# Moving the start addresses of weight and token tiles in a split-precision encoder layer on one Trainium2 core

## The chip, the core and the metric

The kernel runs on one core of one Trainium2 chip. TensorE (PE in the profile) multiplies matrices, and each of its matmuls has a weight load (PEld) ahead of it. VectorE (DVE), ScalarE (ACT) and GpSimd (POOL) work on elements, SyncE (SP) issues most of the DMAs. The operands of all of them lie in SBUF, a memory of 128 partitions; a tile has the same byte address in each partition. Sums of matmuls are collected in PSUM.

The metric is the device time of one execution in microseconds, as the median of some runs.

## The reference: what is computed

One encoder layer (D_MODEL 2048) for two groups of tokens that share all weights: a prompt of 256 and a sample of 32, 288 together.

```python
xn = rmsnorm(x, norm_mix_pre)
u, z, xbc, dt = split(xn @ w_in)              # 1024 | 2048 | 2560 | 32 columns
y_pool = pool_mixer(u)                        # trailing means, w_pool, pool_scale
y_ssd = ssd_mixer(z, xbc, dt)                 # convolution, chunked scan, gate, norm
x = x + rmsnorm(concat[y_pool, y_ssd] @ w_out, norm_mix_post)
up = causal_dwconv(rmsnorm(x, norm_ffn_pre) @ w_up)      # 2 * 5632 columns
x = x + rmsnorm((silu(gate) * value) @ w_down, norm_ffn_post)
```

Outputs are the two new `x` and the new states of pooling, convolutions and scan. All data is float32.

## The kernel before

**Layout.** Features lie on the partitions, the 288 tokens along the free axis. A projection is a sum over blocks of 128 features: the stationary operand is a 128x128 piece of a weight tile, the moving operand a token tile of 128x288.

**Split precision.** TensorE gets rounded operands (`float32r`), so each operand is split into a rounded high part and the rest. A token tile `a` has shape [128, 2, 288]: half 0 is the high part, half 1, which starts 1152 bytes later, the rest. `split_w` (L134) splits a weight tile of 1024 columns: ACT writes `whi` (L146), DVE subtracts and writes `wlo` (L147). `mm3` (L162) then issues three matmuls for each 128x128 piece and 288 tokens:

```python
pe.matmul(out, wh, a[:, 0, :], start=start, stop=False)   # L163
pe.matmul(out, wh, a[:, 1, :], start=False, stop=False)   # L164
pe.matmul(out, wl, a[:, 0, :], start=False, stop=stop)    # L165
```

**Order of the work.** `project` (L167) runs a projection: it fetches raw weights by SP (L131), splits them, and issues the matmuls. The stages follow each other: w_in (token tiles `xn`, about 7 to 337 us of the span), w_pool and w_out (`du`, `mixp`, `mixs`, to 506 us), a normalisation of the whole token axis (about 506 to 550 us), w_up (`hn`) and the two halves of w_down (`fa`), to 1360 us, and the output. Inside w_in and w_out lies the work of the mixers. The narrow 32 columns of `dt` go through `split_narrow` (L151), where high part and rest stand side by side in one 64-column weight piece (L187, L188). A scheduler orders the instructions of each engine when the program is built, from its own model of time.

**Where tiles lie.** The pools are laid out one after the other: `const` (small constants, among them `scan_one` 1152 bytes, `sel`, `pick` and `sel64`, L229 to L239), `wpool` (4 buffers each of `raw`, `whi`, `wlo`), `shift` (one tile of 128 bytes that nothing uses), `apool` (16 token tiles of 2304 bytes), `bpool` (20 tiles of 1152 bytes), and then the pool of a stage (`xin`, `mixer`, `outp` or `ffn`). In the built program every `whi` and `wlo` buffer starts at 224 modulo 256. Buffers are 4096 bytes apart and pieces 512 bytes, so every 128x128 weight piece starts there too. Half 0 of every token tile of the projections (`xn`, `mixs`, `mixp`, `du`, `hn`, `fa`) starts at 96, and half 1 at 224 modulo 256. SBUF is full to 32 bytes in the largest stage.

**Two smaller places.** `state_out` (L684) writes the mixer's states through a tile `so` of its own (L689). The FFN's new state leaves through a tile `fso` (L969).

Of the kernel before, what the change touches and what calls it, by code (L numbers as in the profile page):

```python
# [8 lines left out]
F32 = mybir.dt.float32  # L9
F32R = mybir.dt.float32r  # L10
AF = mybir.ActivationFunctionType
ALU = mybir.AluOpType
AX = mybir.AxisListType
# [3 lines left out]
P = 128  # L17
# [4 lines left out]
NT = NP_ + NS  # L22
# [3 lines left out]
HEADS = 32  # L26
# [3 lines left out]
NX = D_SSD // P  # L30
NF = D_FF // P
# [12 lines left out]
def body(  # L44
# [38 lines left out]
    act, dve, pool, pe, sp = nc.scalar, nc.vector, nc.gpsimd, nc.tensor, nc.sync  # L83
# [10 lines left out]
    const = ctx.enter_context(tc.tile_pool(name="const", bufs=1))  # L94
    wpool = ctx.enter_context(tc.tile_pool(name="wpool", bufs=4))
# [8 lines left out]
    def aux(shape, name):  # L104
        return aux_ps.tile(shape, F32, tag="aux", name=name)
# [4 lines left out]
    def btile(name):  # L110
        return bpool.tile([P, NT], F32, tag="b", name=name)

    def split_from(a, src, scale=None):
# [4 lines left out]
        else:  # L118
# [4 lines left out]
                ),  # L123
            )

    ahead = [0]

    def fetch_w(view, kb, nk, c0, nc_):
# [5 lines left out]
    def split_w(raw, kb, nk, nc_, after=()):  # L134

        out = []
        step = min(nk, 1024 // nc_)
        for k in range(0, nk, step):
            n = min(step, nk - k)
            hi = wpool.tile([P, n, nc_], F32R, tag="hi", name="whi")  # L140
            lo = wpool.tile([P, n, nc_], F32R, tag="lo", name="wlo")
            with ExitStack() as order:
                order.enter_context(tc.high_priority(offset=ahead[0]))
                for ins in after:
                    order.enter_context(tc.issue_after(ins.ins))
                act.activation(hi, raw[:, k : k + n, :], AF.Copy)  # L146
                dve.tensor_tensor(lo, raw[:, k : k + n, :], hi.bitcast(F32), op=ALU.subtract)  # L147
            out.append([(kb + k + i, hi[:, i, :], lo[:, i, :]) for i in range(n)])
        return out
# [17 lines left out]
    def project(view, groups, acts, ksplit, before=None, done=None, spare=0, hold=()):  # L167
# [9 lines left out]
        for i, (kb, n) in enumerate(ksplit):  # L177
            raws = [fetch_w(view, kb, n, c0, w) for c0, w in groups]
            nxt = None
            if before and i + 1 < len(ksplit):  # L180
                nxt = before(*ksplit[i + 1])
            m0 = 0
            for raw, (c0, w) in zip(raws, groups):
                if w < P:
                    for k, both in split_narrow(raw, kb, n, w, after or ()):
                        o = accs[m0][: 2 * w, :]
                        pe.matmul(o, both, acts[k][:, 0, :], start=k == k_first, stop=False)  # L187
                        pe.matmul(o, both, acts[k][:, 1, :], start=False, stop=k == k_last)  # L188
                    continue
                parts = split_w(raw, kb, n, w, ((after or ()) if m0 else ()) + (hold if i else ()))  # L190
                for q, part in enumerate(parts):
                    for m in range(w // P):
                        c = slice(m * P, (m + 1) * P)
                        for k, hi, lo in part:
                            mm3(accs[m0 + m], hi[:, c], lo[:, c], acts[k], k == k_first, k == k_last)
                        if done and i + 1 == len(ksplit) and q + 1 == len(parts):
                            done(m0 + m, accs[m0 + m])
                m0 += w // P
            after = nxt
# [13 lines left out]
    ident = const.tile([P, P], F32, name="ident")  # L213
# [12 lines left out]
    rec = const.tile([P, 16], F32, name="rec")  # L226
    for t in range(16):
        pool.memset(rec[:, t : t + 1], 1.0 / (t + 1))
    scan_one = const.tile([HEADS, NT], F32, name="scan_one")  # L229
    pool.memset(scan_one, 1.0)  # L230
    for c in range(0, NT, 64):
        pool.memset(scan_one[:, c : c + 1], 0.0)
    sel = const.tile([HEADS, 2], F32, name="sel")
    pick = const.tile([HEADS, NX], F32, name="pick")
    id32 = ident[:HEADS, :HEADS]
    dve.tensor_reduce(sel, id32.rearrange("h (t r) -> h r t", r=2), axis=AX.X, op=ALU.add)
    dve.tensor_reduce(pick, id32.rearrange("h (t r) -> h t r", r=2), axis=AX.X, op=ALU.add)
    sel64 = const.tile([HEADS, 2, 64], F32, name="sel64")
    dve.tensor_copy(sel64, sel.unsqueeze(2).broadcast_to([HEADS, 2, 64]))  # L239

    NE = 4
    ebuf = []
    for i in range(NE):
# [120 lines left out]

    mixer = ExitStack()
    mp = mixer.enter_context(tc.tile_pool(name="mixer", bufs=1))
    sc_stage = const.tile([P, 2, 3, NXC], F32, name="sc_stage")
    np_stage = const.tile([P, 2, 15, NU], F32, name="np_stage")
    hist_c = pb[:, 0:60].rearrange("p (r t) -> p r t", t=NXC)
# [43 lines left out]
    def htile(name, n=NT, tag=None):  # L413
        return mp.tile([HEADS, n], F32, tag=tag or name, name=name, bufs={"z": 4}.get(tag, 2) if tag else 1)
# [23 lines left out]
    r = htile("r", tag="z")  # L438
# [42 lines left out]
    for i in range(4):  # L481
        o = btile("bc")
# [201 lines left out]
    def state_out(stage, n, outs, pool_):  # L684

        for s in range(2):
            p_ = aux([n, P], "pso")
            pe.transpose(p_, stage[:, s, :], ident)
            o = pool_.tile([P, P], F32, tag="so", bufs=2, name="so")  # L689
            act.activation(o[:n, :], p_, AF.Copy)  # L690
            sp.dma_start(out=outs[s], in_=o[:n, :])

# [46 lines left out]
    def pool_group(i):  # L739
        raw = fetch_w(wpv, 2 * i, 2, 0, 256)  # L740
        wq = split_w(raw, 0, 2, 256)[0]
        for j in range(2):
            o = acc_ps.tile([P, NT], F32, tag="acc", name="acc")
            c = slice(j * P, (j + 1) * P)
            for k, hi, lo in wq:
                mm3(o, hi[:, c], lo[:, c], uin[2 * i + k], k == 0, k == 1)
            a = op_.tile([P, 2, NT], F32R, name=f"mixp{2 * i + j}")
            split_from(a, o, p_scale[:, 2 * i + j : 2 * i + j + 1])
            mix[2 * i + j] = a
# [46 lines left out]
    for gi in range(2):  # L796
        c = slice(gi * P, (gi + 1) * P)
# [46 lines left out]
    for grp in ((0, 1), (2,), (3,), (4,), (5,), (6,), (7,)):  # L844
        project(
            wov, [(256 * c, 256) for c in grp], mix, [(8, 8), (16, 8), (0, 8)],
            mix_before(grp[0]), lambda m, p_: mix_out(p_),
        )
        if grp[0] < 6:
            for t in range(LATE * (grp[0] - 2) // 4, LATE * (grp[0] - 1) // 4) if grp[0] else ():  # L850
                state_mm(t, *state_in(t))
        elif grp[0] == 6:
            late_in = [state_in(t) for t in range(LATE, NX)]
        if grp[0] == 0:
            sp.dma_start(out=xT, in_=xT_d)
            state_out(sc_stage.rearrange("p s r t -> p s (r t)"), 60, (rows4(new_sconv_p), rows4(new_sconv_s)), op_)
            state_out(np_stage.rearrange("p s r t -> p s (r t)"), 120, (rows4(new_pool_p), rows4(new_pool_s)), op_)
# [10 lines left out]
    for s in range(KD + 1):  # L868
# [3 lines left out]
        if s:  # L872
            t = s - 1
            a = atile("hn")
            hi = act.activation(a[:, 0, :], x1[t], AF.Copy, scale=g_ffn_pre[:, t : t + 1])
            lo = dve.scalar_tensor_tensor(  # L876
                a[:, 1, :], x1[t], g_ffn_pre[:, t : t + 1], a[:, 0, :].bitcast(F32),
                op0=ALU.mult, op1=ALU.subtract,
            )
# [16 lines left out]
    fp = ffn.enter_context(tc.tile_pool(name="ffn", bufs=1))  # L896
# [60 lines left out]
    part = []  # L957
    up_half(0, HALF)
    for m in range(0, KD, 2):
        for p_ in project(wdv[:, 0:HALF, :], [(m * P, 256)], f[:HALF], [(0, 8), (8, 8), (16, 6)]):  # L960
            o = btile("part")
# [3 lines left out]
    for s, o_ in enumerate((new_fconv_p, new_fconv_s)):  # L965
        p_ = aux([2 * NF, 2, P], "pfo")
        for r_ in range(2):
            pe.transpose(p_[:, r_, :], fc_stage[:, s, r_, :], ident)
        so = fp.tile([2 * NF, 2, P], F32, tag="fso", bufs=1, name="fso")  # L969
        act.activation(so, p_, AF.Copy)  # L970
        sp.dma_start(out=o_.rearrange("o b r (t p) -> t (o b r) p", p=P), in_=so)

# [6 lines left out]
    for q in range(4):  # L979
        for b in range(2):  # L980
            t = apool.tile([P, 512], F32, tag="a", name="xr")
# [126 lines left out]
```

## Time and profile before

| what | value |
|---|---|
| median of three runs | 1377.21 us (1376.95 to 1377.78) |
| the profiled execution: its own time | 1377.7 us |
| the profiled execution: span from first to last instruction | 1376.0 us |
| granted TensorE clock, mean | 0.994 |
| PE busy | 1355.0 us (98%) |
| DVE busy | 879.3 us (64%) |
| ACT busy | 670.8 us (49%) |
| POOL busy | 240.8 us (18%) |
| HBM read and written | 234.55 MB and 14.31 MB |

A group of the profile reads: line of the kernel, engine, operation, output<-inputs, shapes, count; then busy time in us and mean ns of one; then the idle time just ahead of them and what ended it. Matmuls overlap each other, so the mean duration of one is more than the time from the start of one to the start of the next, which is called the pitch below. A window row gives for a stretch of the span the busy time of each engine with the number of its instructions in brackets, then the granted clock, the DMA share and GB/s.

### The profile page before, as it was taken

Reading aid. Unit: us, or ns where it says so; the run is one execution under the profiler, and the core shown is the slowest. Engines: PE = TensorE matmul, PEld = TensorE weight load, DVE = VectorE, ACT = ScalarE, POOL = GpSimd, SP = SyncE. Lnnn points to the kernel's source line nnn. Section 1 sums busy time; section 2 is a strip of 40 time slices with the busy share of each in tenths; the row PEclk is TensorE's granted clock in tenths of the full one; section 3 lists DMA queues with packets and bytes.
Section 4 is the critical chain, followed back from the end, with each engine's and each line's share of the span. In section 5 each row is a group of like instructions: output and inputs, shape, how many; then the busy total and the mean of one; then the engine's idle time right before and its main releaser. Section 6 shows DMA issues by size and latency. Waiting matters only on the chain.

```text
span 1376.0 us, 25874 instructions
## 1 busy us (share of the span) xinstructions
PE 1355.0 (98%) x10247; PEld 1333.0 (97%) x10247; DVE 879.3 (64%) x1551; ACT 670.8 (49%) x1013; POOL 240.8 (18%) x394
## 2 busy tenths in 40 slices
PE   8999999999999999999999999999999999999996
PEld 7999999999999998999999999999999999999995
DVE  6898887669544448877667653334766766654443
ACT  6547767546444345644444443334444444454441
POOL 3122211122123310212112100000211211201110
PEclk9999999999999999999999999999999999999998
DMA  8878875455755634766555455555555545476662
GB/s 270 258 194 262 250 207 171 152 187 176 228 179 175 191 106 146 223 176 194 175 157 178 149 169 169 169 170 161 176 161 171 167 156 181 155 230 184 191 186 86
DMA packets 293287, 250.55 MB, mean 182 GB/s; under 512 B 67344, under 2 KB 286458, under 8 KB 293038
## 3 DMA queue, kind: packets, MB, share of 16 engines
q1 hardware_dynamic: 289962, 242.41, 57.8%
q0 software_dynamic: 2320, 3.86, 0.9%
q10 hardware_dynamic: 884, 2.63, 0.5%
q8 instruction: 80, 1.31, 0.4%
q14 instruction: 41, 0.34, 0.1%
HBM read 234.55 MB, written 14.31 MB: 181 GB/s over the span
## 4 chain that ended last, share of the span: by engine, by line
PE 97%; DVE 2%; issue 0%; DMA 0%; ACT 0%; DVEq 0%
PE acc L163 31%; PE acc L165 31%; PE acc L164 30%; PE pst L824 1%; PE py L555 1%; DVE wlo L147 0%; DVE xr L1066 0%; DVE hn L876 0%; PE py L559 0%; PE py L561 0%; PE py L557 0%; DVE xsum L888 0%; DMA xt<-in_x_prompt 0%; PE pt L299 0%; PE pt L301 0%
## 5 line engine op out<-in xcount | busy, mean ns | idle before, releaser
L147 DVE TENSOR_TENSOR wlo<-raw,whi 128x1024 fp32r<-128x1024 f32 (+1 forms) x414 | 493.9, 1194 | 351.2 <-ACT whi L146 349.8
L146 ACT ACTIVATE whi<-raw 128x1024 fp32r<-128x1024 f32 (+1 forms) x414 | 427.1, 1033 | 518.6 <-PE acc L164 424.8
L163 PE MATMUL acc<-hn,whi 128*128 128x288 f32 x1392 | 409.0, 297 | 2.3 <-ACT whi L146 2.3
L165 PE MATMUL acc<-hn,wlo 128*128 128x288 f32 x1392 | 410.0, 296 | 0.9 <-DVE wlo L147 0.9
L164 PE MATMUL acc<-hn,whi 128*128 128x288 f32 x1392 | 405.4, 292 | 0.0
L163 PEld LDWEIGHTS acc<-hn,whi 128*128 128x128 f32 x1392 | 260.9, 188 | 3.5 <-ACT whi L146 3.4
L165 PEld LDWEIGHTS acc<-hn,wlo 128*128 128x128 f32 x1392 | 260.9, 188 | 1.9 <-DVE wlo L147 1.8
L164 PEld LDWEIGHTS acc<-hn,whi 128*128 128x128 f32 x1392 | 262.2, 188 | 0.2 <-DVE hn L876 0.2
L163 PE MATMUL acc<-xn,whi 128*128 128x288 f32 x704 | 210.1, 300 | 0.0
L163 PE MATMUL acc<-fa,whi 128*128 128x288 f32 x704 | 208.5, 296 | 0.0
L165 PE MATMUL acc<-fa,wlo 128*128 128x288 f32 x704 | 207.4, 295 | 0.0
L165 PE MATMUL acc<-xn,wlo 128*128 128x288 f32 x704 | 207.0, 296 | 0.0
L164 PE MATMUL acc<-xn,whi 128*128 128x288 f32 x704 | 206.8, 295 | 0.0
L164 PE MATMUL acc<-fa,whi 128*128 128x288 f32 x704 | 205.3, 292 | 0.0
L163 PEld LDWEIGHTS acc<-xn,whi 128*128 128x128 f32 x704 | 132.6, 189 | 0.7
L164 PEld LDWEIGHTS acc<-xn,whi 128*128 128x128 f32 x704 | 132.8, 189 | 0.3
L164 PEld LDWEIGHTS acc<-fa,whi 128*128 128x128 f32 x704 | 132.3, 188 | 0.0
L163 PEld LDWEIGHTS acc<-fa,whi 128*128 128x128 f32 x704 | 132.3, 188 | 0.0
L165 PEld LDWEIGHTS acc<-xn,wlo 128*128 128x128 f32 x704 | 131.9, 188 | 0.3
L165 PEld LDWEIGHTS acc<-fa,wlo 128*128 128x128 f32 x704 | 131.7, 187 | 0.0
L909 POOL COPY fc_stage<-ebuf 128x4 f32<-128x4 f32 x88 | 27.5, 312 | 506.0 <-DVE ebuf L908 506.0
L905 POOL COPY ebuf<-pf 128x2 f32<-128x2 f32 x88 | 74.5, 847 | 117.9 <-DVE fc L915 54.0
(308 smaller groups left out, 1635.0 us busy)
## 6 DMA issues: line engine op xcount, KB each, us to landing
raw<-in_w_up SPq DMA_DIRECT2D x82, 1024.0 KB, 5.1
raw<-in_w_in SPq DMA_DIRECT2D x40, 1024.0 KB, 5.6
raw<-in_w_down SPq DMA_DIRECT2D x32, 1024.0 KB, 5.4
raw<-in_w_out SPq DMA_DIRECT2D x24, 1024.0 KB, 5.4
raw<-in_w_down SPq DMA_DIRECT2D x16, 768.0 KB, 4.6
gb<-g_d SPq DMA_DIRECT2D x8, 832.0 KB, 4.9
raw<-in_w_up SPq DMA_DIRECT2D x12, 512.0 KB, 3.6
raw<-in_w_in SPq DMA_DIRECT2D x6, 512.0 KB, 6.4
```

The lines of the kernel that those rows point to most:

```text
L146: act.activation(hi, raw[:, k : k + n, :], AF.Copy)
L147: dve.tensor_tensor(lo, raw[:, k : k + n, :], hi.bitcast(F32), op=ALU.subtract)
L163: pe.matmul(out, wh, a[:, 0, :], start=start, stop=False)
L164: pe.matmul(out, wh, a[:, 1, :], start=False, stop=False)
L165: pe.matmul(out, wl, a[:, 0, :], start=False, stop=stop)
L555: pe.matmul(y[c, 0:256], xw[:, 0, c], m[:, j, 0:256], start=True, stop=False)
L824: ins = pe.matmul(st[:, o, :], x_, w, start=i != 1, stop=i != 0)
L905: pool.tensor_copy(e[:, 258:260], pf[:, 4:6, i])
L909: pool.tensor_copy(fc_stage[:, :, :, i], e[:, 256:324].rearrange("p (s c) -> p s c", c=34)[:, :, 0:2])
```

## The change

`split_w` takes its tiles from a new helper, which allocates 1088 columns and uses 1024 of them from the 58th on. The buffers are 4352 bytes, 17 times 256, and the used part begins 58 * 4 = 232 bytes into each:

```diff
+    def wtile(part, n, nc_):
+        t = wpool.tile([P, 1024 + 64], F32R, tag=part, name="w" + part)
+        return t[:, 58 : 58 + n * nc_].rearrange("p (k c) -> p k c", k=n)
...
-            hi = wpool.tile([P, n, nc_], F32R, tag="hi", name="whi")
-            lo = wpool.tile([P, n, nc_], F32R, tag="lo", name="wlo")
+            hi = wtile("hi", n, nc_)
+            lo = wtile("lo", n, nc_)
```

Four constants go from `const` to the mixer's pool, and their nine set-up instructions with them, from the program's start to behind the first projection:

```diff
-    scan_one = const.tile([HEADS, NT], F32, name="scan_one")
+    scan_one = mp.tile([HEADS, NT], F32, name="scan_one")
...
-    sel64 = const.tile([HEADS, 2, 64], F32, name="sel64")
+    sel64 = mp.tile([HEADS, 2, 64], F32, name="sel64")
```

Two tiles of their own become uses of buffers that are there for other things:

```diff
-            o = pool_.tile([P, P], F32, tag="so", bufs=2, name="so")
+            o = pool_.tile([P, NT], F32, tag="sq", bufs=2, name="so")[:, :P]
...
-        so = fp.tile([2 * NF, 2, P], F32, tag="fso", bufs=1, name="fso")
+        so = fp.tile([P, NT], F32, tag="fr", bufs=2, name="fso")[: 2 * NF, : 2 * P].rearrange("p (r c) -> p r c", r=2)
```

In the built program `const` is 1760 bytes shorter, and the buffers of `wpool` start at 0 modulo 256. Every 128x128 weight piece of the projections then starts at 232 modulo 256 (before: 224), half 0 of a token tile at 128 (before: 96) and half 1 at 0 (before: 224). The distance from the start of the weight piece to the start of the token half goes, modulo 256, from 128 to 152 for half 0 and from 0 to 24 for half 1. All matmuls, their shapes and their number stay as they are. The order of PE's instructions is the same but for stretches among its instructions 154 to 1367 (the first projection and the mixer) and 2717 to 2752 (four transposes of `state_out` move behind 34 matmuls).

More of the change, by code (lines that the diff above doesn't have):

```diff
@@ L228, in body @@
         pool.memset(rec[:, t : t + 1], 1.0 / (t + 1))
-    scan_one = const.tile([HEADS, NT], F32, name="scan_one")
[L230 to L237, printed above, removed]
-    sel64 = const.tile([HEADS, 2, 64], F32, name="sel64")
-    dve.tensor_copy(sel64, sel.unsqueeze(2).broadcast_to([HEADS, 2, 64]))
     NE = 4
@@ L366, in body @@
     mp = mixer.enter_context(tc.tile_pool(name="mixer", bufs=1))
+    scan_one = mp.tile([HEADS, NT], F32, name="scan_one")
+    pool.memset(scan_one, 1.0)
+    for c in range(0, NT, 64):
+        pool.memset(scan_one[:, c : c + 1], 0.0)
+    sel = mp.tile([HEADS, 2], F32, name="sel")
+    pick = mp.tile([HEADS, NX], F32, name="pick")
+    id32 = ident[:HEADS, :HEADS]
+    dve.tensor_reduce(sel, id32.rearrange("h (t r) -> h r t", r=2), axis=AX.X, op=ALU.add)
+    dve.tensor_reduce(pick, id32.rearrange("h (t r) -> h t r", r=2), axis=AX.X, op=ALU.add)
+    sel64 = mp.tile([HEADS, 2, 64], F32, name="sel64")
+    dve.tensor_copy(sel64, sel.unsqueeze(2).broadcast_to([HEADS, 2, 64]))
     sc_stage = const.tile([P, 2, 3, NXC], F32, name="sc_stage")
```

## The prediction

> **What bounds the kernel now.** I read the chain of work that ended last first, then windows, then the groups by line with shapes kept apart, and at last the timeline of PE.
>
> ```profile
> ## 4 chain that ended last, share of the span: by engine, by line
> PE 97%; DVE 2%; issue 0%; DMA 0%; ACT 0%; DVEq 0%
> ```
>
> PE carries 97% of the chain. The windows say how it is filled:
>
> ```profile
> 50.00:500.00 450.00, 450.00 (x3462) 436.22 (x3461) 315.52 (x604) 246.36 (x422) 107.75 (x146) 1.00 0.65 195
> 500.00:550.00 50.00, 46.71 (x319) 43.46 (x318) 37.45 (x76) 26.09 (x52) 2.51 (x4) 0.97 0.46 141
> 550.00:1360.00 810.00, 810.00 (x6138) 809.96 (x6136) 485.15 (x789) 366.52 (x488) 114.72 (x185) 1.00 0.57 173
> 600.00:700.00 100.00, 100.00 (x758) 100.00 (x758) 69.21 (x126) 46.85 (x63) 16.75 (x31) 1.00 0.60 179
> ```
>
> The first column after the length is PE. From 50 to 500 us and from 550 to 1360 us it is busy without a gap, at a granted clock of 1.00. Only the start, the normalisation at 500 to 550 us and the last 16 us hold anything else. So the time is a number of matmuls times their pitch. The window from 600 to 700 us has nothing on PE but projections: 100 us / 758 = 131.9 ns from one start to the next. The change alters no count, so it moves the time by what the addresses do to 131.9 ns, and by little else.
>
> How many matmuls that is, and what one costs by line:
>
> ```profile
> L165 PE MATMUL acc<-hn,wlo 128*128 128x288 f32 x1392 | 410.0, 296 | 0.9 <-DVE wlo L147 0.9
> L163 PE MATMUL acc<-hn,whi 128*128 128x288 f32 x1392 | 409.0, 297 | 2.3 <-ACT whi L146 2.3
> L164 PE MATMUL acc<-hn,whi 128*128 128x288 f32 x1392 | 405.4, 292 | 0.0
> L163 PE MATMUL acc<-xn,whi 128*128 128x288 f32 x704 | 210.1, 300 | 0.0
> L163 PE MATMUL acc<-fa,whi 128*128 128x288 f32 x704 | 208.5, 296 | 0.0
> L165 PE MATMUL acc<-fa,wlo 128*128 128x288 f32 x704 | 207.4, 295 | 0.0
> L165 PE MATMUL acc<-xn,wlo 128*128 128x288 f32 x704 | 207.0, 296 | 0.0
> L164 PE MATMUL acc<-xn,whi 128*128 128x288 f32 x704 | 206.8, 295 | 0.0
> L164 PE MATMUL acc<-fa,whi 128*128 128x288 f32 x704 | 205.3, 292 | 0.0
> L163 PE MATMUL acc<-mixs,whi 128*128 128x288 f32 x256 | 76.1, 298 | 0.0
> L165 PE MATMUL acc<-mixs,wlo 128*128 128x288 f32 x256 | 74.6, 295 | 0.0
> L164 PE MATMUL acc<-mixs,whi 128*128 128x288 f32 x256 | 74.5, 292 | 0.0
> L163 PE MATMUL acc<-mixp,whi 128*128 128x288 f32 x128 | 37.9, 296 | 0.0
> L163 PE MATMUL acc_x<-hn,whi 128*128 128x288 f32 x16 | 4.8, 301 | 0.0
> L163 PE MATMUL acc<-du,whi 128*128 128x288 f32 x16 | 4.3, 296 | 0.0
> ```
>
> L163 runs 1392 + 704 + 704 + 256 + 128 + 16 + 16 = 3216 times, L164 and L165 as often: 9648 matmuls, and 9648 x 131.9 ns = 1273 us of the 1376.0 us span. One nanosecond of pitch is 9.65 us.
>
> These rows hold the one sign in this trace that addresses matter. L163 and L164 use the same weight piece, the same shape and the same count. They differ in the token half, which starts at 96 or at 224 modulo 256. Yet L164 is shorter in all four large groups: by 5 ns (hn), 5 (xn), 4 (fa) and 6 (mixs), weighted by the counts 4.9 ns. L165 reads half 0 again and is longer than L164 by 4, 1, 3 and 3 ns, weighted 3.0 ns. The starts show it too:
>
> ```profile
> 699.38 0.30 PE L163 MATMUL acc<-hn,whi 128*128 128x288 f32 x1
> 699.52 0.29 PE L164 MATMUL acc<-hn,whi 128*128 128x288 f32 x1
> 699.64 0.29 PE L165 MATMUL acc<-hn,wlo 128*128 128x288 f32 x1
> 699.77 0.29 PE L163 MATMUL acc<-hn,whi 128*128 128x288 f32 x1
> ```
>
> The steps are 0.14, 0.12 and 0.13 us. The pitch isn't one constant. Some part of it depends on which half is read beside which weights.
>
> **What the change does, part by part.**
>
> *The pitch.* Both streams start elsewhere. Half 0 goes from 96 to 128, half 1 from 224 to 0, the weight piece from 224 to 232 modulo 256. A half is 1152 bytes, nine blocks of 128; before it begins 32 bytes ahead of a multiple of 128 and touches ten such blocks, after it fills nine exactly. The weight load of the next matmul runs beside the present one, so its distance to the token stream counts as well, and that goes from 128 to 152 (half 0) and from 0 to 24 (half 1).
>
> Does the weight load set the pitch? The narrow projection answers, since its pieces have 64 columns:
>
> ```profile
> 28.09 0.30 PE L188 MATMUL acc<-xn,both 128*64 128x288 f32 x1
> 28.88 0.30 PE L188 MATMUL acc<-xn,both 128*64 128x288 f32 x1
> L187 PEld LDWEIGHTS acc<-xn,both 128*64 128x64 f32 x16 | 2.2, 135 | 0.0
> L163 PEld LDWEIGHTS acc<-hn,whi 128*128 128x128 f32 x1392 | 260.9, 188 | 3.5 <-ACT whi L146 3.4
> ```
>
> Between the first two rows lie six starts: 0.79 us / 6 = 131.7 ns, though a weight load takes 135 ns instead of 188. So the load isn't the bound, and at most a small part of the pitch is a collision with it. What can move is the token stream's own cost and its phase against the load.
>
> Bounds for the price. Best end: L163 and L165 come down to L164: 3216 x (4.9 + 3.0) ns = 25.4 us saved. Worst end: L164 and L165 go up to L163: 3216 x (4.9 + 1.9) ns = 21.9 us lost. Nothing in the trace says that the new addresses must fall between these two. The far bound is the load alone: 188 - 135 = 53 ns for 64 columns, thus an estimate of 106 ns for 128, below which no pitch can go; it would be 25.9 x 9.65 = 250 us and is no likely value. I take three quarters of the best end, 19.3 us, which is 2.0 ns for each matmul and a pitch of 129.9 ns. I choose the side of the best end since both halves now fill whole blocks of 128. I stay short of it since the distance 0, which the fastest line has, is given up.
>
> [...]
>
> *Writing the weights at 232.* ACT and DVE write the same elements, shifted.
>
> ```profile
> 50.00:100.00 50.00, 50.00 (x380) 49.83 (x378) 47.01 (x106) 27.70 (x41) 9.95 (x18) 1.00 0.76 223
> 100.00:200.00 100.00, 100.00 (x797) 93.55 (x797) 88.27 (x194) 71.21 (x146) 23.06 (x24) 1.00 0.83 240
> L147 DVE TENSOR_TENSOR wlo<-raw,whi 128x1024 fp32r<-128x1024 f32 x42 | 50.9, 1213 | 5.5 <-ACT whi L146 5.4
> ```
>
> The last row is DVE from 50 to 200 us. There DVE is busy 135.3 of 150 us, and 50.9 us of that is `wlo`. It has 14.7 us to spare, so a `wlo` would have to become 29% longer before DVE is late over this stretch. I cost it at nothing. A `wlo` half as long again would cost 25.5 - 14.7 = 10.8 us here and nothing from 550 us on, where DVE is busy 485 of 810 us.
>
> *The moved constants.*
>
> ```profile
> 1.61 0.17 DVE L236 TENSOR_REDUCE sel<-ident 32x2 f32<-32x32 f32 x1 [1.61 <-POOL ident masks.py:199]
> 1.72 0.17 DVE L237 TENSOR_REDUCE pick<-ident 32x16 f32<-32x32 f32 x1
> 1.82 2.12 DVE L239 COPY sel<-sel 32x128 f32<-32x128 f32 x1
> 2.30 0.33 POOL L230 MEMSET scan_one<- 32x288 f32 x1
> 3.94 0.18 PEld L299 LDWEIGHTS pt<-ident,xt 128*128 128x128 f32 x1 [0.24 <-DMA xt<-in_x_prompt]
> 5.51 0.25 POOL L232 MEMSET scan_one<- 32x1 f32 x5
> ```
>
> At the start, POOL loses 0.33 + 0.25 us and DVE 2.46 us. PE's first input tile comes by DMA, and L299 waits for that, so nothing is gained. They return behind the first projection, where DVE is busy 47.01 of 50 us: 49.5 us with them. PE hides them as long as it is fed; if the stretch gets shorter by 1.5%, to 49.2 us, DVE overhangs by 0.3 us. I charge 0.5 us; uncovered it would be 2.5 us.
>
> *The shared buffers and the order.* `so` now waits for slots of `sq`, `fso` uses those of `fr`. Nothing of the projections reads them, the transposes that feed `so` only move behind 34 matmuls, and PE has no gap from 50 to 500 us and from 550 us on that such a wait could lengthen. Cost nothing; a missed slot would hold ACT for one POOL addition:
>
> ```profile
> L609 POOL TENSOR_TENSOR msum<-msum,sq 128x288 f32<-128x288 f32 x13 | 15.1, 1165 | 86.0 <-ACT sq L608 84.4 <-DMA raw<-in_w_out 1.6
> ```
>
> That is 1.2 us, twice at most, and `whi` is made further ahead than that.
>
> **Sum.** -19.3 + 0.5 = -18.8 us on the span: 1376.0 - 18.8 = 1357.2 us. The profiled execution itself took 1377.7 us, 1.7 us around its span, so 1358.9 us; the median of the runs is 0.5 us lower, so 1358.4 us. I forecast 1358 us.
>
> **The rivals.**
>
> *A larger gain.* If whole blocks help L164 as much as the two others, each matmul saves about 5 ns instead of 2: 48 us, 1329 us. For it: the steps of 0.12 us show that PE can start the next matmul sooner than the mean. Against it: a step of 0.14 us stands beside each, so the short one may only catch up. [...]
>
> *Nothing happens.* The classes of 4.9 and 3.0 ns may be an effect of the phase in the triple, not of the addresses, since L163 and L165 read the very same half and still differ. Then the pitch stays at 131.9 ns and the time at 1377 us, with at most 2.5 us from the moved constants. The narrow pieces' 131.7 ns speak for it. [...]
>
> *Slower.* L164 may be the quick one exactly because its token half and its weight piece start at the same phase, 224 and 224. The change puts 24 bytes between them and leaves no pair at distance 0. Then L164 rises by 4.9 ns: 3216 x 4.9 = 15.8 us, 1393 us; if all become as long as L163, 21.9 us, 1399 us. It decides as soon as the pitch in 600 to 700 us is above 131.9 ns, that is with fewer than 758 matmuls there. For it: the weight load starts within 0.01 us of the matmul, so phases do meet. Against it: half 0 moves away from 128, at which the slow lines stand.
>
> **How the numbers follow.** The forecast case (5 to 35 us less) gets 0.45, the larger gain 0.18, nothing 0.13, slower 0.24. A measurement of this kernel can tell about 0.2%, 2.8 us, from no change. Of the case in which nothing happens I put 0.09 within that, 0.03 below and 0.01 above. So faster 0.45 + 0.18 + 0.03 = 0.66, same 0.09, slower 0.25. Faster cases hold most of the chance. The range leaves out a tenth at either side: the larger gain up to 55 us (1322 us), and the slower case up to 17 us (1394 us).
>
> **What would show it.** In the window from 600 to 700 us 770 matmuls instead of 758; L163 and L165 near 294 ns; PE still without a gap from 50 to 500 us. L163 and L164 equal but the count at 758 would mean that the classes were only phase. Fewer than 758 is the slower rival. Gaps of PE at `wlo` between 50 and 200 us would be the writes.

## The result and the profile after

The changed kernel takes 1368.97 us (median, 1368.53 to 1369.71), beside 1377.08 us for the kernel before. The ratio is 0.9941 with a 95% interval of 0.9924 to 0.9959: 8 us or 0.6% faster. The forecast was 1358 us, a saving of 19 us: the direction was right, the saving much smaller. The profiled execution took 1368.83 us, its span is 1367.1 us, 8.9 us shorter than before.

In the changed file `mm3` stands five lines further down: L168, L169 and L170 are what L163, L164 and L165 were. The chain and the windows of the profile after:

```profile
PE 97%; DVE 2%; DMA 0%; issue 0%; ACT 0%; SPq 0%; DVEq 0%
50.00:500.00 450.00, 450.00 (x3474) 435.93 (x3473) 316.51 (x608) 247.38 (x422) 119.91 (x152) 1.00 0.64 196
600.00:700.00 100.00, 100.00 (x765) 100.00 (x765) 70.41 (x129) 48.09 (x65) 16.65 (x32) 1.00 0.59 179
```

PE still has no gap there, and the granted clock is 1.00 as before. From 600 to 700 us there are now 765 matmuls instead of 758: 130.7 ns from one start to the next instead of 131.9. The forecast asked for 770.

Which stages got shorter? Two windows of each kernel hold w_out and, with the wait ahead of it, the FFN. Before:

```profile
337.00:506.00 169.00, 169.00 (x1259) 166.09 (x1258) 79.90 (x122) 71.56 (x105) 50.86 (x75) 1.00 0.57 176
512.00:1360.00 848.00, 844.71 (x6366) 842.28 (x6366) 517.40 (x857) 386.78 (x530) 116.11 (x187) 1.00 0.56 171
```

After:

```profile
337.00:505.00 168.00, 168.00 (x1258) 165.08 (x1258) 80.26 (x122) 71.80 (x105) 50.89 (x75) 1.00 0.57 177
511.00:1351.00 840.00, 836.71 (x6365) 834.15 (x6366) 517.42 (x857) 386.53 (x529) 112.90 (x187) 1.00 0.55 173
```

Nearly the same number of matmuls takes 848 us and then 840 us, and 169 us and then 168 us. The last matmul of w_in starts at 336.9 us before and at 336.8 us after. So the FFN has nearly all of the gain, w_out 1 us, and w_in ends no earlier.

The groups by line of the profile after show how the pitch got shorter:

```profile
L170 PE MATMUL acc<-hn,wlo 128*128 128x288 f32 x1392 | 413.0, 298 | 1.0 <-DVE wlo L152 1.0
L168 PE MATMUL acc<-hn,whi 128*128 128x288 f32 x1392 | 403.8, 293 | 2.3 <-ACT whi L151 2.2
L169 PE MATMUL acc<-hn,whi 128*128 128x288 f32 x1392 | 403.0, 290 | 0.0
```

Before they stood at 297 (first), 292 (second) and 296 ns (third line). The first is 4 ns shorter, the second 2 ns shorter, the third 2 ns longer. The forecast had the first and the third near 294 ns; they are at 293 and 298 ns. The three don't come to one level, there is a new pattern. The starts show it as well:

```profile
699.60 0.29 PE L169 MATMUL acc<-hn,whi 128*128 128x288 f32 x1
699.72 0.30 PE L170 MATMUL acc<-hn,wlo 128*128 128x288 f32 x1
699.86 0.29 PE L168 MATMUL acc<-hn,whi 128*128 128x288 f32 x1
699.99 0.29 PE L169 MATMUL acc<-hn,whi 128*128 128x288 f32 x1
```

The steps are 0.12, 0.14 and 0.13 us: a short step is still followed by a long one.

The trace holds starts in whole nanoseconds. For the tables below I took the step from each projection matmul to the next and averaged it by line; steps of 160 ns or more and steps to other matmuls are left out. From 600 to 1200 us, in ns:

```
                     first line  second  third   mean
before                  135.4     129.2   132.1   132.2
after                   131.7     127.5   134.2   131.1
```

The mean of such steps is 1.1 ns lower in this stretch. From the first matmul to 337 us it is 131.93 ns before and 131.48 ns after, only 0.45 ns lower. No run shows why w_in gains less.

### The profile page after: what moved, and what is told of

It is laid out like the page before. It is cut to its first block, busy times and chain, and to the rows that moved or that the text cites. A ratio compares the mean times of both kernels' runs of the same rounds, so it can differ in the third digit from the quotient of the medians.

```text
span 1367.1 us, 25869 instructions
## 1 busy us (share of the span) xinstructions
PE 1346.4 (98%) x10247; PEld 1323.9 (97%) x10247; DVE 877.5 (64%) x1551; ACT 670.6 (49%) x1013; POOL 248.7 (18%) x394
## 4 chain that ended last, share of the span: by engine, by line
PE 97%; DVE 2%; DMA 0%; issue 0%; ACT 0%; SPq 0%; DVEq 0%
PE acc L170 31%; PE acc L168 30%; PE acc L169 30%; PE pst L828 1%; PE py L559 1%; DVE wlo L152 0%; DVE xr L1070 0%; DMA xt<-in_x_prompt 0%; DVE hn L880 0%; PE py L563 0%; PE py L565 0%; PE py L561 0%; DVE xsum L892 0%; PE pt L294 0%; DVE mg L875 0%
## 5 line engine op out<-in xcount | busy, mean ns | idle before, releaser
L170 PE MATMUL acc<-hn,wlo 128*128 128x288 f32 x1392 | 413.0, 298 | 1.0 <-DVE wlo L152 1.0
L168 PE MATMUL acc<-hn,whi 128*128 128x288 f32 x1392 | 403.8, 293 | 2.3 <-ACT whi L151 2.2
L169 PE MATMUL acc<-hn,whi 128*128 128x288 f32 x1392 | 403.0, 290 | 0.0
L168 PEld LDWEIGHTS acc<-hn,whi 128*128 128x128 f32 x1392 | 260.0, 188 | 3.5 <-ACT whi L151 3.4
L170 PEld LDWEIGHTS acc<-hn,wlo 128*128 128x128 f32 x1392 | 261.1, 188 | 2.1 <-DVE wlo L152 1.7
L169 PEld LDWEIGHTS acc<-hn,whi 128*128 128x128 f32 x1392 | 261.3, 188 | 0.2 <-DVE hn L880 0.2
L170 PE MATMUL acc<-fa,wlo 128*128 128x288 f32 x704 | 209.3, 297 | 0.0
L170 PE MATMUL acc<-xn,wlo 128*128 128x288 f32 x704 | 209.3, 299 | 0.0
L168 PE MATMUL acc<-xn,whi 128*128 128x288 f32 x704 | 208.3, 298 | 0.0
L169 PE MATMUL acc<-xn,whi 128*128 128x288 f32 x704 | 206.8, 295 | 0.0
L168 PE MATMUL acc<-fa,whi 128*128 128x288 f32 x704 | 206.2, 293 | 0.0
L169 PE MATMUL acc<-fa,whi 128*128 128x288 f32 x704 | 204.3, 290 | 0.0
L168 PEld LDWEIGHTS acc<-xn,whi 128*128 128x128 f32 x704 | 132.8, 189 | 0.5
L169 PEld LDWEIGHTS acc<-xn,whi 128*128 128x128 f32 x704 | 132.9, 189 | 0.4
L170 PEld LDWEIGHTS acc<-xn,wlo 128*128 128x128 f32 x704 | 132.5, 189 | 0.5
L168 PEld LDWEIGHTS acc<-fa,whi 128*128 128x128 f32 x704 | 132.2, 188 | 0.0
L169 PEld LDWEIGHTS acc<-fa,whi 128*128 128x128 f32 x704 | 132.2, 188 | 0.0
L170 PEld LDWEIGHTS acc<-fa,wlo 128*128 128x128 f32 x704 | 132.1, 188 | 0.0
L919 DVE SCALAR_TENSOR_TENSOR fc<-ebuf,pf,fc 128x290 f32<-128x290 f32 x176 | 90.5, 516 | 3.4 <-ACT fc L917 0.6
```

The costliest lines, as they stand in the source:

```text
L919: dve.scalar_tensor_tensor(c, e[:, r_ : r_ + 290], pf[:, r_, i : i + 1], c, op0=ALU.mult, op1=ALU.add)
```

## The experiments

The theory on record said that whole blocks of 128 bytes in the token stream bring the gain (block theory), and that the distance to the weight piece counts too. I set four theories against each other: the blocks, the weights' own start, the distance alone, and the other edits of the change. All kernels up to the seventh are the changed kernel with other start addresses; PE, ACT, DVE and SP run the very same order of instructions in them.

**1. The old addresses in the changed kernel**

```diff
-    shift_t = shift.tile([P, 32], F32, name="shift_t")
+    shift_t = shift.tile([P, 24], F32, name="shift_t")
...
-        return t[:, 58 : 58 + n * nc_]...
+        return t[:, 56 : 56 + n * nc_]...
```

> All other edits of the change (moved constants, shared buffers, instruction order), but weights at 224 and token halves at 96 and 224 modulo 256, as before. If the addresses alone bring the gain (all three address theories): 758 matmuls in the window from 600 to 700 us and 1377 us. If the other edits bring it: 765 matmuls or fewer, and 1369 us.

Measured: 1377.74 us, ratio 1.0004 (0.9992 to 1.0016). The window from 600 to 700 us:

```profile
600.00:700.00 100.00, 100.00 (x759) 100.00 (x758) 69.54 (x127) 48.05 (x64) 17.21 (x32) 1.00 0.59 179
```

759 matmuls, beside 758 before the change. The moved constants, the shared buffers and the other order of instructions are worth nothing beyond the interval, about 2 us either way. This kernel and the changed one differ in addresses alone, so the addresses bring the gain.

**2. Only the tokens moved** (weights at 56 columns, so 224; `shift_t` as after)

> Token halves at 128 and 0 as after the change, weights at 224 as before. Block theory (the prediction's choice: whole blocks of 128 bytes in the token stream): the full gain, 765 matmuls from 600 to 700 us, 1369 us. Weight-start theory (232 matters, whatever the tokens do): no gain, 758 and 1377 us. Distance theory (only the distance of the token half to the weight piece counts, here 160 and 32): another value than both, it can't say which.

Measured: 1377.37 us, ratio 1.0002 (0.9993 to 1.0012).

```profile
600.00:700.00 100.00, 100.00 (x761) 100.00 (x760) 69.53 (x125) 47.34 (x64) 16.72 (x31) 1.00 0.59 177
```

The tokens fill whole blocks, and there are 761 matmuls, not 765. The mean step from 600 to 1200 us is 131.9 ns, beside 132.2 before and 131.1 after the change. The block theory, which asked for the full gain, falls.

**3. Only the weights moved** (weights at 58 columns, so 232; `shift_t` of 24 columns)

> Weights at 232 as after the change, token halves at 96 and 224 as before. Block theory: no gain, 758 matmuls from 600 to 700 us, 1377 us. Weight-start theory: the full gain, 765 and 1369 us. Distance theory (distances 120 and 248): another value than both.

Measured: 1378.58 us, ratio 1.0009 (1.0000 to 1.0019).

```profile
600.00:700.00 100.00, 100.00 (x758) 100.00 (x758) 69.50 (x126) 47.52 (x63) 15.35 (x31) 1.00 0.59 179
```

758 matmuls, and a mean step of 132.2 ns as before: 232 as such is no good start either. Neither half of the change shortens the time alone. The lines have yet another pattern here: 130.4, 134.6 and 131.7 ns, with the second line, the shortest before, now the longest.

**4. The same distances at other addresses** (weights at 50 columns, so 200; `shift_t` of 24 columns)

> Token halves at 96 and 224 as before, weights at 200, so that the distances are 152 and 24 as after the change, at other addresses. Distance theory: the full gain, 765 matmuls from 600 to 700 us and 1369 us, with the same mean durations by line as after the change. Block theory and weight-start theory: no gain, 758 and 1377 us.

Measured: 1368.66 us, ratio 0.9937 (0.9922 to 0.9951).

```profile
600.00:700.00 100.00, 100.00 (x765) 100.00 (x764) 70.39 (x129) 47.58 (x65) 16.62 (x32) 1.00 0.60 179
L170 PE MATMUL acc<-hn,wlo 128*128 128x288 f32 x1392 | 413.1, 298 | 1.4 <-DVE wlo L152 1.4
L168 PE MATMUL acc<-hn,whi 128*128 128x288 f32 x1392 | 403.9, 293 | 2.3 <-ACT whi L151 2.2
L169 PE MATMUL acc<-hn,whi 128*128 128x288 f32 x1392 | 403.0, 290 | 0.0
```

The whole gain with tokens where they had always been, and the same 298, 293 and 290 ns by line. Of the four theories only the distance from the weight piece to the token half is left.

**5 and 6. All distances in one trace.** The start of the weight tiles goes through all 32 multiples of 8, with tokens as after (5) and as before (6). `turn` counts the calls of the loop in `split_w`:

```diff
-        return t[:, 58 : 58 + n * nc_]...
+        o = 2 * (13 * turn[0] % 32)
+        return t[:, o : o + n * nc_]...
...
+            turn[0] += 1
```

> Token halves at 128 and 0; the start of the weight tiles goes through all 32 multiples of 8 modulo 256, from one pair of tiles to the next, so that one trace holds the pitch at every distance. Distance theory: the pitch, sorted by the weights' start, has its low near 232 (131.1 ns) and differs by several ns between starts. Block theory: flat, the pitch is 131.1 ns at every start of the weights.

> The same sweep with token halves at 96 and 224. Distance theory: the same curve as with tokens at 128 and 0, moved by 32 bytes, with 132.2 ns at 224 and 131.1 ns at 200. Block theory: flat at 132.2 ns.

Measured (one execution each): 1381.89 and 1382.99 us, beside 1376.99 us of the kernel before on the same chip. The mean step of the three lines by the weights' start, in ns, from 50 us on; in the second row the start is 32 lower, so that a column has one distance:

```
tokens 128 and 0, start        240     184      72     152  ...   232  ...   224  ...   128      16     144
                            130.11  131.25  131.65  131.66     132.47     132.74     133.34  134.37  134.51
tokens 96 and 224, start       208     152      40     120  ...   200  ...   192  ...    96     240     112
                            130.12  131.16  131.87  131.68     132.23     132.82     133.39  134.27  134.58
```

Moved by 32 bytes, the two curves agree within 0.25 ns at every one of the 32 starts (correlation 0.99; unmoved it is -0.13). The distance theory holds over the whole circle. The curve has no smooth shape: starts 8 bytes apart differ by up to 2.9 ns (240 and 248).

The distance of the change has 132.5 ns within the sweep and 131.2 ns where all tiles have it. The tile ahead explains most of it: a tile of the sweep has eight pieces, and those at 232 begin with 132.7 ns in the first two and end with 131.3 ns in the last two (131.9, 128.0 and 133.9 ns by line, close to the 131.7, 127.5 and 134.2 ns of the changed kernel). So at this distance the steps have come down by the last six of a tile's 24 matmuls. Those at 224 have not settled by the end of a tile: 132.8 ns in the last two pieces, beside 131.9 ns in run 2. A sweep's means are a first guide only.

**7. The best distance of the sweep**

```diff
-        return t[:, 58 : 58 + n * nc_]...
+        return t[:, 60 : 60 + n * nc_]...
```

> The changed kernel with the weights 8 bytes further, at 240 (distances 144 and 16). In both sweeps this distance had the lowest mean step between matmul starts, 130.2 ns, beside 132.5 and 132.3 ns for the change's own distance in the same sweeps and 131.2 ns for it in the changed kernel. Distance theory, if the sweep's order holds when all tiles have one distance: 130.2 ns or less, 10 us or more below the changed kernel, 1359 us or less. If a tile's pitch also hangs on the distance of the tile ahead of it (phase carried over): anywhere between 1359 and 1378 us. Block theory: 1369 us.

Measured: 1362.35 us (1359.39 to 1367.67, four runs), ratio 0.9907 (0.9884 to 0.9931). The profiled execution took 1359.39 us.

```profile
600.00:700.00 100.00, 100.00 (x771) 100.00 (x771) 70.19 (x127) 47.41 (x65) 18.32 (x32) 1.00 0.59 182
L170 PE MATMUL acc<-hn,wlo 128*128 128x288 f32 x1392 | 408.3, 294 | 0.9 <-DVE wlo L152 0.9
L169 PE MATMUL acc<-hn,whi 128*128 128x288 f32 x1392 | 405.9, 293 | 0.0
L168 PE MATMUL acc<-hn,whi 128*128 128x288 f32 x1392 | 399.6, 290 | 2.4 <-ACT whi L151 2.4
```

771 matmuls in the window, a pitch of 129.7 ns. All four runs are below all of the changed kernel's; its interval and that of the change overlap by a hair (0.9924 to 0.9931). From 600 to 1200 us the mean step is 130.0 ns, 1.1 below that of the change, which was itself 1.1 below that of the kernel before. So eight bytes further bring as much again in the pitch, and in the medians somewhat more than half as much again, while both halves still fill whole blocks.

**8. Short weight loads** (all projection matmuls but the first and last three of each sum; the kernel leaves out three quarters of the outputs of these matmuls)

```diff
     def mm3(out, wh, wl, a, start, stop):
+        n = P if start or stop else 32
+        out, wh, wl = out[:n, :], wh[:, :n], wl[:, :n]
```

> In the changed kernel all projection matmuls but the first and last three of each sum load only 32 of the 128 weight columns, so three quarters of the outputs are incomplete; the token streams of 288 stay. [...]

The question was whether the load that runs beside a matmul takes time from its token stream, called the collision theory here; then a shorter load would shorten the pitch of 131 ns.

Measured: 1366.89 us (one execution).

```profile
600.00:700.00 100.00, 100.00 (x763) 84.61 (x762) 69.79 (x127) 47.54 (x64) 17.38 (x32) 1.00 0.60 183
L171 PEld LDWEIGHTS acc<-hn,whi 128*32 128x32 f32 x1218 | 131.8, 108 | 27.6 <-DVE hn L882 0.6
```

A load takes 108 ns instead of 188, and there are 763 matmuls against 765. Between two short ones the step is 131.1 ns, as between two whole ones after the change. The collision theory, put in this way, falls: with three quarters of the columns of the load left out the step gets no shorter.

**9. High parts at 240, rests through all starts** (the rest of the edit as in 5)

```diff
+        o = 60 if part == "hi" else 2 * (13 * turn[0] % 32)
...
```

> High parts of the weights at 240, the rests go through all 32 multiples of 8 modulo 256. Collision theory: line 164's matmul runs beside the load of the rest, so its step changes most with the rest's start; lines 163 and 165 run beside loads of high parts, which keep their distance, and change by less than 2 ns. Phase theory (each matmul's step hangs on how the one ahead of it ended): all three lines change alike. A start other than 240 may give a mean below 130 ns.

Measured: 1376.32 us (one execution). By the rest's start, the mean steps run from 127.8 to 136.7 ns in the first line, from 127.5 to 136.2 in the second and from 130.4 to 136.8 in the third. The first line's matmul runs beside the load of a high part (in the traces before and after, from 600 to 1200 us, each load starts 2 to 5 ns after the matmul ahead of its own). That load kept its distance in all cases, and yet the first line changes by 8.9 ns. So the step of a matmul hangs on what went ahead of it, as the phase theory says. No start has a mean below 130 ns; it is lowest, 130.3 ns, with the rest at 240 as well.

**10. Starts 4 bytes past the multiples of 8** (the sweep of 5 with `o` one more)

> The sweep with token halves at 128 and 0, with the weights at 4 bytes past each multiple of 8. If only 8-byte steps matter, each start has the mean of one of its two neighbours in the first sweep, 130.2 to 134.5 ns. If single words matter, the curve goes on between them and may have a lower point. ACT and DVE write these tiles too: if an odd word costs them time, their mean for a tile of 1024 columns rises above 1057 and 1224 ns.

Measured: 1386.11 us (one execution). The means run from 131.2 ns (228) to 135.9 ns (20), beyond both ends of what the neighbours allow (224 and 232 have 132.7 and 132.5 ns, 16 and 24 have 134.4 and 133.1 ns), so single words matter. No odd start is as good as 240. ACT and DVE take 1059 and 1225 ns for a tile at an odd word, beside 1057 and 1224 ns before:

```profile
L155 ACT ACTIVATE whi<-raw 128x1024 fp32r<-128x1024 f32 x390 | 412.6, 1059 | 490.8 <-PE acc L173 420.1 <-issue 60.8 <-DMA out<-ho 3.5
L156 DVE TENSOR_TENSOR wlo<-raw,whi 128x1024 fp32r<-128x1024 f32 x390 | 477.7, 1225 | 336.6 <-ACT whi L155 335.2
```

**11. The sweep with short loads** (5 and 8 together)

> The sweep of the weights' start with token halves at 128 and 0, together with the loads of 32 columns (all projection matmuls but the first and last three of each sum; three quarters of the outputs stay incomplete). With whole loads the mean pitch by start went from 130.2 to 134.5 ns. Length theory (the distance acts all along a load, as the streams pass each other): with a quarter of the load the spread falls to about a quarter, 1 ns or less, around the 131.4 ns of the run with 32 columns at one distance. Start theory (the distance acts where load and stream begin): the spread stays at 3 to 4 ns, with the same order of starts, 240 low and 16 and 144 high.

Measured: 1368.57 us (one execution), beside 1381.12 us of the kernel before on the same chip. Between two short loads the means by start run from 129.9 to 133.1 ns, a spread of 3.2 ns against 4.4 with whole loads; their average falls from 132.7 to 131.4 ns. The order is another: the lowest is 0, and 240 is above the average with 131.9. Neither theory holds. The spread didn't fall to a quarter, and the order did not stay. With a quarter of the load the step still changes with the distance, by these 3.2 ns, and other distances are good.

**12. Streams of 256 tokens** (all projection matmuls but the first and last three of each sum; the kernel leaves out the sample's tokens in them)

```diff
     def mm3(out, wh, wl, a, start, stop):
+        n = NT if start or stop else NP_
+        out, a = out[:, :n], a[:, :, :n]
```

> The changed kernel with token streams of 256 instead of 288 columns in all projection matmuls but the first and last three of each sum (the sample's outputs are incomplete). [...]

The question was what the 131.1 ns consist of.

Measured: 1268.9 us (one execution), beside 1381.12 us of the kernel before on the same chip. From 600 to 700 us there are 831 matmuls, of both lengths:

```profile
600.00:700.00 100.00, 100.00 (x831) 100.00 (x830) 73.01 (x134) 52.28 (x70) 19.54 (x36) 1.00 0.57 184
```

From one matmul with 256 columns to the next the step is 118.8 ns, 12.3 ns less than 131.1. A cost in proportion to the columns would be an estimate of 32/288 of 131.1 ns, 14.6 ns less. The step lost less than that, as with a fixed part in each matmul's cost, but as distances move the mean step by 2 ns either way in the sweeps (130.1 to 134.5 ns), this doesn't settle it. The weight loads of 128 columns still take 188 to 190 ns there, beside 187 to 189 before, so the step fell without a shorter load.

## Why the prediction was right or wrong

- **PE's pitch sets the time, all else is cover:** right. PE has no gap from 50 to 500 us, and the count in one window went with the time: 758 and 1377 us, 765 and 1369 us, 771 and 1359 us (the profiled execution). Run 2 falls out of this with 761 and 1377 us. Its profile has a slower start, 294 matmuls in the first 50 us instead of 304; whether its other executions had that too isn't known.
- **The pitch depends on addresses; L163 against L164 is the sign of it:** right. Experiment 1 against the changed kernel differs in addresses alone, and has all of the 8 us.
- **Nothing happens, because the lines' differences are only phase in the triple:** the pitch did fall. But the reason given is half right: the differences are a phase, which the addresses set. In run 3 the same second line is the longest (134.6 ns, before 129.2), and in experiment 9 the distance of one load moves all three lines, by 8.9, 8.7 and 6.4 ns.
- **"I choose the side of the best end since both halves now fill whole blocks of 128":** wrong, and the step that failed first. Experiment 2 has the whole blocks and no gain (ratio 1.0002); experiment 4 has the gain without them (0.9937). What counts is the distance between weight piece and token half, which the prediction named but gave no price of its own. From the trace before, a good distance could not be told from a bad one. So the right direction was luck: in run 5 the mean step is longer than that of the old distance (132.1 ns at start 0) at 25 of the 32 starts, and the change's own is among them there.
- **The size, 2.0 ns for each matmul or 19.3 us:** wrong, the term that was mis-sized; the span lost 8.9 us. (Three quarters of 25.4 us are 19.1 us; the 19.3 us are 9648 times the rounded 2.0 ns.) The pitch in the window fell by 1.2 ns, and 9648 times that would be 11.6 us. It fell by 0.45 ns in w_in, and the start was slower there. The first 50 us before and after, by PE and the other engines:

```profile
0.00:50.00 50.00, 44.92 (x304) 41.28 (x305) 34.25 (x70) 29.32 (x47) 15.83 (x60) 1.00 0.85 266
```

```profile
0.00:50.00 50.00, 45.09 (x299) 41.44 (x300) 31.40 (x67) 29.29 (x47) 14.75 (x54) 1.00 0.83 261
```

  299 matmuls had started by then against 304. The new order of instructions isn't the cause: with it, the traces of runs 1 to 4 have 306, 294, 306 and 298. The differences between the lines were taken for savings that each line could have by itself. They are not: a short step comes with a long one behind it (127.5 and 134.2 ns after), and experiment 9 shows that one load's distance moves all three lines. Only the mean of the three is a price.
- **A larger gain, 5 ns for each matmul:** no start in the sweeps of 5 and 6 has it, nor has run 7 with 130.0 ns from 600 to 1200 us. A step of 127.5 ns stands beside one of 134.2, as the prediction's argument against this rival had it.
- **Writing at 232, moved constants, shared buffers at about nothing:** right. ACT and DVE take 1059 and 1225 ns for a tile of 1024 columns, against 1057 and 1224 before; experiment 1 puts all the rest at a ratio of 1.0004.
- **The load isn't the bound:** right, by experiment 8, where the load takes 108 ns instead of 188 and the step stays at 131.1 ns. But "at most a small part of the pitch is a collision with it" gave too little weight to the load's place: its distance moves the pitch by 4.4 ns within a sweep, its length by 1.3 ns on the average of all starts.
- **Slower, because no pair stays at distance 0:** wrong. The second line got shorter at 24 (127.5 ns) than it was at 0 (129.2 ns). For an arbitrary distance a loss was the nearer case, though, by the 25 of 32 starts above.

What stays open is where in a matmul the distance acts, and whether the weight piece that counts is the matmul's own or the next one's, since in runs 1 to 4 and 7 all pieces start alike. Its effect isn't in proportion to the length of the load (a spread of 3.2 ns with a quarter of it, 4.4 ns with the whole, experiment 11), and it is carried from one matmul to the next (8.9 ns in the first line, experiment 9). What the rest of the pitch consists of is open as well: by experiment 12 a column costs 12.3 / 32 ns, so that 288 of them would be an estimate of 111 of the 131.1 ns.

## What to carry to other kernels

Where matmuls of one shape run without a gap and the next weights are loaded beside each (here the load starts 2 to 5 ns after the matmul), the difference of the start addresses of weights and moving tiles is a variable to try; here the mean step goes from 130.1 ns at the best to 134.5 ns at the worst multiple of 8, and moving both operands by 32 bytes changes it by no more than 0.25 ns. A sweep in one trace, with another start for each tile, finds candidates; but the tile ahead counts (the change's distance has 132.5 ns in the sweep and 131.2 ns where all tiles have it), so a candidate must be run with all tiles alike. Moving only one of two operands may show nothing in the time, as in runs 2 and 3 (ratios 1.0002 and 1.0009), though both together gain (0.9941).

## What was not expected of the hardware

- The step from matmul to matmul depends on the distance of the two operands' starts modulo 256, down to one 4-byte word: 130.1 to 135.9 ns in the sweeps, the same curve within 0.25 ns when both operands move by 32 bytes.
- At the change's own distance, a weight load of 32 columns (108 ns) instead of 128 (188 ns) beside each matmul leaves the step at 131.1 ns.
- At the change's own distance the steps have three means by line, 131.7, 127.5 and 134.2 ns, which hold within 0.3 ns in every 100 us from 650 to 1250 us, and are the same to 0.01 ns from 600 to 1200 us in run 4, at other addresses with the same distances.
